# Modulation half vectors on TensorE, four weight chunks at a time in column groups of the array

## The chip, the cores and the metric

One core of a Trainium2 chip runs the whole program. The metric is the device time of one execution in microseconds (us), as the median of several runs. TensorE appears in the profile as PE (matmuls) and PEld (weight loads), VectorE as DVE, ScalarE as ACT, GpSimd as POOL, and SyncE, which issues most transfers, as SP.

## The reference

Two layers over 512 latent tokens and 256 context tokens of width 1024. Every sub-layer norms its input, multiplies by one plus a scale vector and adds a shift vector; those vectors ("modulation") come from a conditioning vector c through one large matrix, once for the latents and once for the context.

```python
silu_c = jax.nn.silu(c)
silu_cc = jax.nn.silu(c_ctx)
for i in range(DEPTH):
    m_lat = (silu_c @ ada_w[i] + ada_b[i]).reshape(b, N_SUBLAYERS, N_MOD, 1, d)
    m_ctx = (silu_cc @ ada_w[i] + ada_b[i]).reshape(N_SUBLAYERS, N_MOD, 1, d)
    h = norm_modulate(x_lat, norm_g[i, 0], m_lat[:, 0, 0], m_lat[:, 0, 1])
    x_lat = x_lat + MACARON_WEIGHT * m_lat[:, 0, 2] * swiglu(h, ffn_w_in[i, 0], ffn_w_out[i, 0])
```

After the first feed-forward come a token mixer (a short convolution in layer 0, attention in layer 1) and a second feed-forward. The output is a final norm of the latent tokens. All data are float32.

## The kernel before

Tokens lie along the free dimension and the 1024 features along the partitions, in 8 chunks of 128 (`KC`). Each weight and each normed activation is split into a high and a low float32r part (`split`, L178 on ACT and L179 on DVE), and a product is three matmuls (`mm3`, L388 to L390): high by high, high by low, low by high. Normed activations are the tiles `h` (high) and `hl` (low), weights `wh` and `wl`, cut from a landed block `raw`.

A modulation vector has 1024 entries and is made as two halves of 512, numbered `hm`; (0,2) and (0,3) are the two halves of layer 0's first scale vector, (0,0) and (0,1) those of its first shift vector. These four are needed before the first norm can end, and are made first:

- `ada_load` (L197 on) issues eight transfers on SP, one weight piece `adw` [128, 512] for each chunk k of c. The pieces share ten buffers in turn, so a later transfer waits until the matmul on the buffer's previous piece is done.
- `ada_direct` (L207 to L218) makes a half on TensorE, for (0,2), (0,0) and (0,3). Eight float32 matmuls (L211) with the activated conditioning vector `silu_c[:, k, :]`, two columns (latents, context), as the stationary operand sum into two rows of one PSUM bank. ACT copies the two rows out (`adr`, L214), four transposes turn them to 128 partitions (L217, PSUM tile `ps_S`, of which there is one buffer), and `ada_put` adds the bias (L193) into `mods`. It is a generator: it yields behind each matmul, and the caller places the steps between other work of TensorE.
- `ada_split` (L226 on) makes (0,1) with its sum over k on DVE (`acc`, L222 and L224), for the latents and then for the context, and sums over partitions with four matmuls against ones (L235).

The order of work in this stretch is written by hand: TensorE's and SP's order is the program order throughout, and DVE's and ACT's too until `boot_order.close()`. The top level runs (0,2) on TensorE, loads x, then the squares of x (L306 to L310), their sum over partitions (L335, L336), the root (`rsqrt`, L318 to L322), with the steps of (0,0) between. Then scale (L341), t = x * scale * r (L361), h (L381, on ACT) and hl (L368) for the first four chunks. The first feed-forward's `first` (its three first chunks of hidden columns) calls `boot` ahead of each of its first eleven steps of three matmuls, which places one matmul of (0,3) before each of the first eight; later calls place the rest of (0,3), the column sums of (0,1), and the whole norm of the context tokens (x of the context is `xc`).

Of the kernel before, what the change touches and what calls it, by code (L numbers as in the profile page):

```python
# [9 lines left out]
F32 = mybir.dt.float32  # L10
F32R = mybir.dt.float32r
BF16 = mybir.dt.bfloat16
AF = mybir.ActivationFunctionType
ALU = mybir.AluOpType
# [3 lines left out]
P = 128  # L18
# [29 lines left out]
def backbone(ctx: ExitStack, tc: tile.TileContext, a: dict, out: bass.AP):  # L48
# [10 lines left out]

    # ---------------------------------------------------------- PSUM  # L60
    bank = {}
# [13 lines left out]

    # ---------------------------------------------------------- constants
    packed = ctile("packed", [P, sum(n for _, n in VECTORS)])
# [29 lines left out]

    # ---------------------------------------------------------- weights
    # Each entry of the stream is one transfer of `units` stationary blocks [P, k chunks, P].
    stream = []  # L110
# [69 lines left out]

    # ---------------------------------------------------------- adaLN vectors
    silu_c = ctile("silu_c", [P, KC, 2])
    ada_tasks = []
    ada_done = set()

    def ada_setup():
        act.activation(silu_c, cvec, AF.Sigmoid)
        dve.tensor_mul(silu_c, silu_c, cvec)

    def ada_put(i, hm, src_ps, vs):  # L190
# [16 lines left out]
    def ada_direct(i, hm, loaded):  # L207
        """Steps of one half vector on TensorE, for the ones that the first norm waits for."""
        ps = ptile("B")
        for k, w in enumerate(loaded):  # L210
            pe.matmul(ps[:2, :], silu_c[:, k, :], w, start=(k == 0), stop=(k == KC - 1))  # L211
            yield
        row = tmp.tile([P, NL], F32, name=f"adr{hm}", tag="t")
        act.activation(row[:2, :512], ps[:2, :], AF.Copy)  # L214
        pt = ptile("S", (P, 4, 2))
        for j in range(4):
            pe.transpose(pt[:, j, :], row[:2, j * P : (j + 1) * P], ident[:2, :2])  # L217
        ada_put(i, hm, pt, range(2))  # L218

# [6 lines left out]
    def ada_split(i, hm, loaded):  # L226
        """A half vector with its sum over k on VectorE, for one token group after the other."""
        acc = apool.tile([P, 2, 512], F32, name=f"acc{i}_{hm}", tag="acc")
        for v in range(2):
            for k, w in enumerate(loaded):  # L230
                ada_add(acc[:, v, :], w, k, v, k == 0)
                yield
            pt = ptile("S", (P, 4, 2))
            for j in range(4):
                pe.matmul(pt[:, j, v : v + 1], acc[:, v, j * P : (j + 1) * P], ones_f, start=True, stop=True)  # L235
            ada_put(i, hm, pt, [v])
            yield
# [47 lines left out]
    def mod_groups(i, m):  # L285
        """Token groups that use modulation vector m of layer i: past the last keys and values, only the latents."""
        return 1 if (i == 1 and m >= 5) else 2
# [4 lines left out]

    # ---------------------------------------------------------- activations
    x_lat = xp.tile([P, KC, NL], F32, name="xl", tag="xl")
# [20 lines left out]
    def rsqrt(r, ps, rows, n, dim):  # L315
        """r = 1/sqrt(ps / dim): the tables' value and one Newton step."""
        y = tmp.tile([P, NL], F32, name="y", tag="t")[:rows, :n]
        act.activation(y, ps, AF.Ln, scale=1.0 / dim)  # L318
        act.activation(y, y, AF.Exp, scale=-0.5)
        dve.tensor_mul(r, y, y)  # L320
        dve.scalar_tensor_tensor(out=r, in0=ps, scalar=-0.5 / dim, in1=r, op0=ALU.mult, op1=ALU.mult)
        dve.scalar_tensor_tensor(out=r, in0=r, scalar=1.5, in1=y, op0=ALU.add, op1=ALU.mult)  # L322

    def parts_of(src, n, dim):
        """src + eps * dim / P, whose sum over the partitions is dim times the mean square plus eps."""
        th = tmp.tile([P, NL], F32R, name="th", tag="th", bufs=1)[:, :n]
# [5 lines left out]
    def rstd_of(th, tl, n, dim, r):  # L332
        """r = 1/sqrt(sum over partitions of th + tl / dim + eps), on every partition."""
        ps = ptile("S")[:, :n]
# [57 lines left out]
    def banks(grp, count, own=False):  # L392
        """PSUM for `count` outputs of one token group."""
        v, off, n = grp
# [9 lines left out]
    def project(grp, units, ps, interleave=False, mid=None, hooks={}):  # L404
        """ps[u] = unit u's columns applied to the normed tokens of one group."""
        v, off, n = grp
# [16 lines left out]
    def out_steps(groups, gh, gl, npart, after):  # L423
        """Steps of x += gate * (w_out applied to the npart chunks in gh/gl).

        `after` is the norm that follows the last part: it starts on the first group while the
        second is still being summed; the second group's norm is left in `pending`."""

# [54 lines left out]

    # ---------------------------------------------------------- sub-layers
    def gated(gp, count, name):
        return ([gp.tile([P, NT], F32R, name=f"{name}{z}{f}", tag=f"g{z}{f}") for f in range(count)] for z in "hl")

    def ffn(gp, i, s, groups, after, boot=None):
# [12 lines left out]
        def first(lat, cxt):  # L501
            """The first three chunks: the latents' part begins with half of the k chunks."""
            units = [w_get(1), w_get(1)]
# [16 lines left out]
        def opening(main, other):  # L520
            """The first three chunks: the main group's part covers the norm of the other group."""
            units = [w_get(), w_get(), w_get()]
# [87 lines left out]
    def attention(gp, i, s, after):  # L610
# [7 lines left out]
        with tc.tile_pool(name="rope", bufs=1) as rp, psum(A=4, B=2, S=1, Q=1):  # L618
# [4 lines left out]
            def turned(dst, p, g, n):  # L623
                """dst = the rotation of p * g; g[:, 1] is g with its halves swapped."""
                w = tmp.tile([P, NL], F32, name="hw", tag="t")[:, :n]
# [36 lines left out]

            # Heads are normed behind their projections, `n` of them in the course of one.
            lat, cxt = BOTH
# [174 lines left out]

    # ---------------------------------------------------------- program  # L840
    for i in range(2):
# [13 lines left out]
    with tc.tile_pool(name="apool", bufs=1) as apool, tc.tile_pool(name="g0", bufs=1) as gp, psum(A=4, B=3, S=1):  # L855
# [4 lines left out]
        scale = ada_direct(0, 2, ada_load(gp, 0, 2))  # L860
        for _ in range(KC):
            next(scale)
# [3 lines left out]
        shift = ada_direct(0, 0, ada_load(gp, 0, 0))  # L866
        for _ in range(3):
            next(shift)
        for m in range(KC):
            sq_add(m, 0, NL)  # L870
        parts = norm_parts(lat)
        r = norm_rstd(lat, *parts)
        for _ in range(3):
            next(shift)
        next(scale, None)
        for _ in range(2):
            next(shift)
        scale_vec(0, 0, slice(0, 4))
# [8 lines left out]
        def boot_steps():  # L887
            scale = ada_direct(0, 3, ada_load(gp, 0, 3))
            shift = ada_load(gp, 0, 1)
            for m in range(KC):  # L890
                nc.sync.dma_start(xc[m], a["x"][m, :, NL:])
            for _ in range(KC):
                next(scale)
                yield
# [55 lines left out]
def _layout(i):  # L950
# [20 lines left out]
    w = arr("attn_w_qkv")[0].reshape(KC, P, 6, 2, P)  # L971
    # The halves that rotate into each other lie 64 partitions apart, both axes in each.
    qk = w.reshape(KC, P, 6, 2, 2, 2, NF).swapaxes(4, 5).reshape(w.shape).transpose(2, 1, 3, 0, 4)
# [27 lines left out]
```

## Time and profile before

| | us |
|---|---|
| median of 3 runs | 2629.04 |
| lowest and highest run | 2628.71, 2629.2 |
| profiled execution, first to last instruction (span) | 2627.3 |
| TensorE busy in it | 2595.5 |
| half vectors made by L211, first to last matmul start | 4.6 to 44.7 |

The profile shows one execution. Its span is 1.7 us under the median of the runs, which holds what lies around the first and last instruction as well. Busy time of TensorE says that it had a matmul in flight, not that the array was full. A float32 matmul appears as two instructions, a float32r matmul as one.

### The profile page before, as it was taken

How to read it: one execution, taken by the hardware profiler on the slowest of the kernel's cores; microseconds unless marked ns; L12 is line 12 of the kernel's file. 1: busy time of each engine (PE TensorE's matmuls, PEld its weight loads, DVE VectorE, ACT ScalarE, POOL GpSimd, SP SyncE). 2: the span in 40 equal slices, each digit the busy share in tenths (PEclk: the TensorE clock that was granted, in tenths of full speed). 3: DMA queues.
4: the chain of work that ended last, by engine and by line, in shares of the span. 5: the costliest groups of instructions: out<-in, count | busy, mean ns of one | idle time of the engine just before them, and what ended most of it. 6: DMA issues, size and time to landing. Idle time of an engine off the chain costs nothing.

```text
span 2627.3 us, 38843 instructions
## 1 busy us (share of the span) xinstructions
PE 2595.5 (99%) x16500; PEld 2302.0 (88%) x16500; DVE 1579.6 (60%) x2692; ACT 870.5 (33%) x1398; POOL 0.7 (0%) x6
## 2 busy tenths in 40 slices
PE   8999999999999999999999999999999999999998
PEld 3888888888888888888888888888888799999998
DVE  6856566569656674555756745443337887644445
ACT  3423222234213432222323422221125785422222
POOL 0000000000000000000000000000000000000000
PEclk9999999999999999999999999999999999999999
DMA  6333232232323032332323233321112201223221
GB/s 242 137 122 106 93 121 97 89 113 74 120 81 121 33 126 86 110 113 97 121 89 125 82 110 108 122 77 53 64 65 73 81 1 34 86 97 107 97 87 43
DMA packets 69566, 249.57 MB, mean 95 GB/s; under 512 B 5776, under 2 KB 8976, under 8 KB 56336
## 3 DMA queue, kind: packets, MB, share of 16 engines
q1 hardware_dynamic: 52112, 184.17, 20.0%
q10 hardware_dynamic: 17280, 62.92, 6.8%
q8 instruction: 129, 2.11, 0.3%
q14 instruction: 45, 0.37, 0.0%
HBM read 244.97 MB, written 2.10 MB: 94 GB/s over the span
## 4 chain that ended last, share of the span: by engine, by line
PE 93%; DVE 4%; ACT 2%; DMA 0%; issue 0%; SPq 0%; DVEq 0%; ACTq 0%
PE ps_A L388 19%; PE ps_A L389 18%; PE ps_A L390 18%; PE ps_B L388 11%; PE ps_B L389 11%; PE ps_B L390 11%; PE ps_S L268 1%; DVE wl L179 1%; DVE hl L368 1%; DVE t L361 1%; PE ps_B L211 1%; ACT pr L764 1%; PE ps_T L780 0%; DVE ssq L310 0%; PE ps_O L390 0%
## 5 line engine op out<-in xcount | busy, mean ns | idle before, releaser
L388 PE MATMUL ps_A<-h,wh 128*128 128x512 f32 (+1 forms) x1624 | 604.5, 372 | 0.3 <-ACT h L381 0.3
L389 PE MATMUL ps_A<-hl,wh 128*128 128x512 f32 (+1 forms) x1624 | 601.7, 370 | 0.4 <-DVE hl L368 0.4
L390 PE MATMUL ps_A<-h,wl 128*128 128x512 f32 (+1 forms) x1624 | 601.7, 370 | 0.1
L178 ACT ACTIVATE wh<-raw 128x1024 fp32r<-128x1024 f32 (+2 forms) x342 | 339.0, 993 | 642.9 <-PE ps_B L389 626.0
L179 DVE TENSOR_TENSOR wl<-raw,wh 128x1024 fp32r<-128x1024 f32 (+2 forms) x342 | 389.5, 1141 | 234.6 <-ACT wh L178 230.7
L388 PE MATMUL ps_B<-h,wh 128*128 128x256 f32 (+1 forms) x1672 | 479.7, 287 | 0.0
L389 PE MATMUL ps_B<-hl,wh 128*128 128x256 f32 (+1 forms) x1672 | 478.4, 286 | 0.4 <-DVE hl L368 0.2
L390 PE MATMUL ps_B<-h,wl 128*128 128x256 f32 (+1 forms) x1672 | 477.6, 286 | 0.0
L388 PEld LDWEIGHTS ps_A<-h,wh 128*128 128x128 f32 x1624 | 305.9, 188 | 60.3 <-issue 6.0
L390 PEld LDWEIGHTS ps_A<-h,wl 128*128 128x128 f32 x1624 | 305.8, 188 | 56.5 <-DVE wl L179 0.6
L389 PEld LDWEIGHTS ps_A<-hl,wh 128*128 128x128 f32 x1624 | 306.0, 188 | 54.5 <-DVE hl L368 1.8
L389 PEld LDWEIGHTS ps_B<-hl,wh 128*128 128x128 f32 x1672 | 314.9, 188 | 5.8 <-DVE hl L368 1.2
L388 PEld LDWEIGHTS ps_B<-h,wh 128*128 128x128 f32 x1672 | 315.1, 188 | 4.6
L390 PEld LDWEIGHTS ps_B<-h,wl 128*128 128x128 f32 x1672 | 315.1, 188 | 2.5
L224 DVE SCALAR_TENSOR_TENSOR acc<-aw,silu_c,acc 128x512 f32<-128x512 f32 x392 | 278.0, 746 | 16.0 <-DMA aw<-in_ada_w 14.6
L388 PE MATMUL ps_A<-gh,wh 128*128 128x512 f32 (+1 forms) x704 | 255.8, 363 | 0.0
L389 PE MATMUL ps_A<-gl,wh 128*128 128x512 f32 (+1 forms) x704 | 255.7, 363 | 0.0
L390 PE MATMUL ps_A<-gh,wl 128*128 128x512 f32 (+1 forms) x704 | 255.3, 363 | 0.0
L441 DVE SCALAR_TENSOR_TENSOR xl<-ps_A,gat,xl 128x512 f32<-128x512 f32 (+1 forms) x192 | 126.5, 671 | 203.2 <-PE ps_A L390 203.1
L390 PE MATMUL ps_B<-gh,wl 128*128 128x256 f32 x704 | 199.2, 283 | 0.0
L389 PE MATMUL ps_B<-gl,wh 128*128 128x256 f32 x704 | 199.2, 283 | 0.0
L388 PE MATMUL ps_B<-gh,wh 128*128 128x256 f32 x704 | 199.1, 283 | 0.0
(203 smaller groups left out, 3103.2 us busy)
## 6 DMA issues: line engine op xcount, KB each, us to landing
raw<-in_ffn_w_in SPq DMA_DIRECT2D x88, 1024.0 KB, 4.8
aw<-in_ada_w ACTq DMA_DIRECT2D x120, 512.0 KB, 3.2
raw<-in_ffn_w_out SPq DMA_DIRECT2D x24, 1024.0 KB, 4.9
raw<-in_ffn_w_out SPq DMA_DIRECT2D x32, 640.0 KB, 3.9
adw<-in_ada_w SPq DMA_DIRECT2D x32, 256.0 KB, 5.4
raw<-in_conv_w_in SPq DMA_DIRECT2D x8, 1024.0 KB, 4.9
raw<-in_attn_w_qkv SPq DMA_DIRECT2D x6, 1024.0 KB, 4.8
aw<-in_ada_w SPq DMA_DIRECT2D x8, 512.0 KB, 3.4
```

Of the source, the lines that this page charges most:

```text
L178: act.activation(dsth, src, AF.Copy)
L179: dve.tensor_tensor(out=dstl, in0=src, in1=dsth.bitcast(F32), op=ALU.subtract)
L211: pe.matmul(ps[:2, :], silu_c[:, k, :], w, start=(k == 0), stop=(k == KC - 1))
L224: dve.scalar_tensor_tensor(out=acc, in0=w, scalar=silu_c[:, k, v : v + 1], in1=acc, op0=ALU.mult, op1=ALU.add)
L268: pe.matmul(pt[:, j, v : v + 1], pc[:, j * P : (j + 1) * P], ones_b, start=(n == 0), stop=(n == 2))
L361: dve.scalar_tensor_tensor(out=t, in0=xs(m, off, n), scalar=scl[:, m, v : v + 1], in1=r, op0=ALU.mult, op1=ALU.mult)
L368: dve.scalar_tensor_tensor(out=hl[m][:, off : off + n], in0=t, scalar=mods[i][:, 3 * s, m, v : v + 1], in1=hs.bitcast(F32), op0=ALU.add, o ...
L388: pe.matmul(ps, wh, xh, start=first, stop=False)
L389: pe.matmul(ps, wh, xl, start=False, stop=False)
L390: pe.matmul(ps, wl, xh, start=False, stop=last)
L441: dve.scalar_tensor_tensor(out=x, in0=p[:, :n], scalar=gat[:, m0 + u, v : v + 1], in1=x, op0=ALU.mult, op1=ALU.add)
L764: act.activation(pr, sc, AF.Exp, bias=sm[:, 1:2], scale=rq[:, blk, h : h + 1], accum_out=sm[:, 2:3])
```

## The change

`silu_c` is copied into a zeroed tile `silu_p` [128, 8, 32], which borrows the buffer of the last low part `hl7`. `ada_direct` gives the matmul of chunk k the 32 array columns from 32 * (k % 4) on, so that it writes the 32 rows of the same number in PSUM; chunks k and k + 4 sum into the same rows. It yields after four matmuls instead of one. ACT copies all 128 rows, four full 128x128 transposes turn them, a reduce on DVE adds the four partial sums (columns 32 g + c for the two c), and `ada_put` adds the bias from that sum. The callers take a step where they took four.

```diff
     def ada_setup():
         act.activation(silu_c, cvec, AF.Sigmoid)
         dve.tensor_mul(silu_c, silu_c, cvec)
+        silu_p.append(xp.tile([P, KC, 32], F32, name="silu_p", tag="hl7"))
+        dve.memset(silu_p[0], 0.0)
+        dve.tensor_copy(silu_p[0][:, :, :2], silu_c)
...
         ps = ptile("B")
         for k, w in enumerate(loaded):
-            pe.matmul(ps[:2, :], silu_c[:, k, :], w, start=(k == 0), stop=(k == KC - 1))
-            yield
+            g = 32 * (k % 4)
+            pe.matmul(ps[g : g + 32, :], silu_p[0][:, k, :], w, start=(k < 4), stop=(k >= 4), tile_position=(0, g), skip_group_check=True)
+            if k % 4 == 3:
+                yield
         row = tmp.tile([P, NL], F32, name=f"adr{hm}", tag="t")
-        act.activation(row[:2, :512], ps[:2, :], AF.Copy)
-        pt = ptile("S", (P, 4, 2))
+        act.activation(row, ps, AF.Copy)
+        pt = ptile("S", (P, 4, P))
         for j in range(4):
-            pe.transpose(pt[:, j, :], row[:2, j * P : (j + 1) * P], ident[:2, :2])
-        ada_put(i, hm, pt, range(2))
+            pe.transpose(pt[:, j, :], row[:, j * P : (j + 1) * P], ident)
+        sums = tmp.tile([P, 4, 2], F32, name=f"ads{hm}", tag="ads", bufs=1)
+        dve.tensor_reduce(out=sums, in_=pt.rearrange("p j (g c) -> p j c g", g=4)[:, :, :2, :], axis=AX.X, op=ALU.add)
+        ada_put(i, hm, sums, range(2))
...
-        for _ in range(KC):
+        for _ in range(2):
             next(scale)
...
-        for _ in range(3):
-            next(shift)
+        next(shift)
         for m in range(KC):
             sq_add(m, 0, NL)
         parts = norm_parts(lat)
         r = norm_rstd(lat, *parts)
-        for _ in range(3):
-            next(shift)
         next(scale, None)
-        for _ in range(2):
-            next(shift)
+        next(shift)
...
-            for _ in range(KC):
-                next(scale)
+            for k in range(KC):
+                if k % 4 == 3:
+                    next(scale)
                 yield
```

Line numbers move by 4 from `ada_load` on and by 8 behind `ada_direct`: L211 becomes L216, the transposes L217 become L223, the reduce is L225, L335 is L343, and L388 to L390 are L396 to L398.

The first place is TensorE's queue around the sum of squares (L335, L336), where the names are those of the sections above. Before:

```order
L211 MATMUL ps_B<-adw_2_161,silu_c 2x512
L335 MATMUL ps_S<-th,ones_r 128x512
L336 MATMUL ps_S<-tl,ones_r 128x512
L211 MATMUL ps_B<-adw_3_163,silu_c 2x512
L211 MATMUL ps_B<-adw_4_165,silu_c 2x512
L211 MATMUL ps_B<-adw_5_167,silu_c 2x512
L217 MATMUL ps_S<-ident,adr_216 128x2 x4
L211 MATMUL ps_B<-adw_6_169,silu_c 2x512
L211 MATMUL ps_B<-adw_7_171,silu_c 2x512
L217 MATMUL ps_S<-ident,adr_233 128x2 x4
```

The same place now:

```order
L216 MATMUL ps_B<-adw_2_164,silu_p 32x512
L216 MATMUL ps_B<-adw_3_166,silu_p 32x512
L343 MATMUL ps_S<-th,ones_r 128x512
L344 MATMUL ps_S<-tl,ones_r 128x512
L223 MATMUL ps_S<-ident,adr_217 128x128 x4
L216 MATMUL ps_B<-adw_4_168,silu_p 32x512
L216 MATMUL ps_B<-adw_5_170,silu_p 32x512
L216 MATMUL ps_B<-adw_6_172,silu_p 32x512
L216 MATMUL ps_B<-adw_7_174,silu_p 32x512
L223 MATMUL ps_S<-ident,adr_238 128x128 x4
```

The matmul of k=3 has moved ahead of the sum of squares, and those of k=4 and k=5 behind the transposes of (0,2).

The second place is TensorE's queue in the first chunk of the feed-forward, where (0,3) is worked in. Before, from the first matmul of (0,3):

```order
L211 MATMUL ps_B<-adw_0_298,silu_c 2x512
L388 MATMUL ps_A<-h_252,wh_0_244 128x512
L389 MATMUL ps_A<-hl_253,wh_0_244 128x512
L390 MATMUL ps_A<-h_252,wl_0_245 128x512
L211 MATMUL ps_B<-adw_1_300,silu_c 2x512
L388 MATMUL ps_A<-h_252,wh_1_246 128x512
L389 MATMUL ps_A<-hl_253,wh_1_246 128x512
L390 MATMUL ps_A<-h_252,wl_1_247 128x512
L211 MATMUL ps_B<-adw_2_302,silu_c 2x512
```

Now, from the end of the third step of three:

```order
L396 MATMUL ps_A<-h_259,wh_0_251 128x512
L397 MATMUL ps_A<-hl_262,wh_0_251 128x512
L398 MATMUL ps_A<-h_259,wl_0_252 128x512
L216 MATMUL ps_B<-adw_0_305,silu_p 32x512
L216 MATMUL ps_B<-adw_1_307,silu_p 32x512
L216 MATMUL ps_B<-adw_2_309,silu_p 32x512
L216 MATMUL ps_B<-adw_3_311,silu_p 32x512
L396 MATMUL ps_A<-h_259,wh_1_253 128x512
L397 MATMUL ps_A<-hl_262,wh_1_253 128x512
L398 MATMUL ps_A<-h_259,wl_1_254 128x512
```

Before, one matmul of (0,3) stood ahead of each of the first eight steps; now four stand behind the third step and four behind the seventh. SP's and ACT's queues keep their order, and DVE's gains the memset, the copy and three reduces, each directly ahead of the adds that it feeds.

More of the change, by code (lines that the diff above doesn't have):

```diff
@@ L182, in backbone @@
     silu_c = ctile("silu_c", [P, KC, 2])
+    silu_p = []
     ada_tasks = []
```

## The prediction

> **What bounds the kernel now.** I read the page first, for the engine that sets the end.
>
> ```profile
> span 2627.3 us, 38843 instructions
> PE 2595.5 (99%) x16500; PEld 2302.0 (88%) x16500; DVE 1579.6 (60%) x2692; ACT 870.5 (33%) x1398; POOL 0.7 (0%) x6
> PE 93%; DVE 4%; ACT 2%; DMA 0%; issue 0%; SPq 0%; DVEq 0%; ACTq 0%
> ```
>
> The third line is the chain of work that ended last: TensorE nearly throughout. A microsecond taken from TensorE's queue therefore comes off the end, unless another chain is then late at a later join. The change touches only the first 50 us, so next I read the timeline of that stretch (start, length, engine, line, operation; in brackets the idle time before it and what ended it).
>
> ```profile
> 12.01 5.12 SPq L203 DMA_DIRECT2D adw<-in_ada_w  x8
> 17.46 4.42 PE L211 MATMUL ps_B<-adw,silu_c 128*2 128x512 f32 x6 [4.36 <-DMA adw<-in_ada_w]
> 21.81 0.50 PE L335 MATMUL ps_S<-th,ones_r 128*128 128x512 f32 x1
> 22.47 2.74 PE L211 MATMUL ps_B<-adw,silu_c 128*2 128x512 f32 x6
> 25.50 0.38 PE L217 MATMUL ps_S<-ident,adr 2*128 2x2 f32 x4 [0.29 <-DVE r L321]
> 25.80 1.88 PE L211 MATMUL ps_B<-adw,silu_c 128*2 128x512 f32 x4
> 27.78 0.59 ACT L214 ACTIVATE adr<-ps_B 2x512 f32<-2x512 f32 x1 [3.40 <-PE ps_B L211]
> 28.42 0.40 PE L217 MATMUL ps_S<-ident,adr 2*128 2x2 f32 x4 [0.74 <-ACT adr L214]
> 28.86 0.23 DVE L193 TENSOR_TENSOR mods<-ps_S,packed 128x4 f32<-128x4 f32 x2 [1.06 <-PE ps_S L217]
> 31.01 0.73 PE L389 MATMUL ps_A<-hl,wh 128*128 128x512 f32 x1 [0.44 <-DVE hl L368]
> ```
>
> Seen here: the shift vector (0,0) is the long chain. Its sums (L211) end at 27.68, then come ACT's copy, the transposes and the add at 28.86; h and hl start from it, and TensorE's steady work from hl at 31.01. Each float32 matmul is two instructions (x6 is three matmuls). Warm, six take 2.74, so their starts lie (2.74-0.59)/5 = 0.43 us apart.
>
> Behind that, the other two vectors share the queue with the first feed-forward chunks.
>
> ```profile
> 35.07 1.02 PE L211 MATMUL ps_B<-adw,silu_c 128*2 128x512 f32 x2
> 36.02 0.50 PE L388 MATMUL ps_A<-h,wh 128*128 128x512 f32 x1
> 36.90 1.02 PE L211 MATMUL ps_B<-adw,silu_c 128*2 128x512 f32 x2
> 38.68 3.90 DVE L224 SCALAR_TENSOR_TENSOR acc<-adw,silu_c,acc 128x512 f32<-128x512 f32 x5
> 39.80 2.17 SPq L203 DMA_DIRECT2D adw<-in_ada_w  x2
> 44.72 0.75 DVE L224 SCALAR_TENSOR_TENSOR acc<-adw,silu_c,acc 128x512 f32<-128x512 f32 x1 [1.05 <-DMA adw<-in_ada_w]
> 47.50 0.40 PE L389 MATMUL ps_A<-hl,wh 128*128 128x512 f32 x1
> 47.73 0.39 PE L390 MATMUL ps_A<-h,wl 128*128 128x512 f32 x1
> 47.96 0.95 PE L235 MATMUL ps_S<-ones_f,acc 128*128 128x1 f32 x8
> 48.77 0.48 PE L388 MATMUL ps_A<-h,wh 128*128 128x512 f32 x1
> ```
>
> An f32r matmul costs TensorE 47.73-47.50 = 0.23. One step with a modulation matmul takes 36.90-35.07 = 1.83, so that matmul costs 1.83-3x0.23 = 1.14, of which 0.86 is its own two instructions and the rest the turn to and from it. Between 31 and 46 us TensorE carries seven of them. At 47.96 it reaches the column sums of vector (0,1) (L235), whose sum DVE finished at 44.72+0.75 = 45.47: there is 2.4 us of room for TensorE to come earlier before it must wait for DVE. DVE in turn waited for the last weight piece, which SP issues at 39.80+2.17-0.33 = 41.64, when the k=5 matmul of (0,3) frees its buffer.
>
> The granted clock is the third thing that carries the sum.
>
> ```profile
> 17.46:20.87 3.41, 3.41 (x5) 0.50 (x6) 2.01 (x3) 0.72 (x1) 0.00 (x0) 0.50 1.06 398
> 20.87:31.11 10.24, 8.47 (x27) 2.07 (x25) 6.05 (x15) 5.04 (x10) 0.00 (x0) 1.00 1.02 399
> 31.11:34.53 3.42, 3.42 (x6) 0.96 (x7) 3.29 (x6) 1.57 (x4) 0.00 (x0) 0.50 0.54 198
> 34.53:44.77 10.24, 10.24 (x30) 3.11 (x28) 8.48 (x12) 2.27 (x3) 0.00 (x0) 1.00 0.47 160
> ```
>
> The number before the last two is the clock: half in 17.46 to 20.87 and again in 31.11 to 34.53, full otherwise. It changes on a grid of 3.41 us, so every cold matmul here costs twice the warm one, and how busy TensorE is in one such stretch settles the next.
>
> **The change, part by part.** *Setup.* A memset of 128x256 and a small copy on DVE, between the silu product and the first matmul.
>
> ```profile
> 0.83 0.17 DVE L90 MEMSET ones_r<- 128x128 f32 x1 [0.83 <-PEq L990]
> 3.00 0.18 DVE L188 TENSOR_TENSOR silu_c<-silu_c,packed 128x16 f32<-128x16 f32 x1 [1.80 <-ACT silu_c L187]
> 4.55 8.54 PE L211 MATMUL ps_B<-adw,silu_c 128*2 128x512 f32 x16 [4.55 <-DMA adw<-in_ada_w]
> ```
>
> Twice the memset plus a copy like L188 is 0.34+0.18 = 0.52, from 3.18 to 3.7; the first matmul waits for its weights until 4.55. Cost 0; it would show only from 0.85 us more.
>
> *A group of four matmuls.* No row of before has column groups, so I bound it. Above: nothing overlaps, eight starts, 8x0.43 = 3.44 warm. Below: the four run side by side, 2x0.43 = 0.86. I take the middle case: TensorE starts its instructions in program order in all these rows, and a matmul's second instruction starts 0.43 after its first into the same rows of PSUM; the next matmul's first can therefore run beside the previous one's second, not earlier. That makes five steps, 5x0.43 = 2.15 warm, plus 0.10 at each turn (36.02-35.07-2x0.43 = 0.09 today). [...]
>
> *Row, transposes, reduce.* ACT copies 128 rows rather than 2, the transposes are 128x128, and a reduce stands ahead of the adds.
>
> ```profile
> 83.49 0.58 ACT L494 ACTIVATE sg<-ps_A 128x512 f32<-128x512 f32 x1
> 2100.45 0.88 PE L780 MATMUL ps_T<-ident,pr 128*128 128x128 f32 x6 [0.47 <-ACT pr L767]
> L780 PE MATMUL ps_T<-ident,pr 128*128 128x128 f32 x192 | 27.8, 275 | 1.8 <-DVE p L179 1.1 <-ACT pr L767 0.5
> L729 DVE TENSOR_SCALAR rq<-ps_S 128x32 f32<-128x32 f32 x1 | 0.2, 184 | 0.0
> ```
>
> The copy costs the same (0.58 against 0.59). Six transposes take 0.88, so four take 0.275+3x0.12 = 0.64 against 0.40: +0.24. The reduce reads the 32 columns that L729 reads: 0.18, with the step to the next dependent instruction 0.22; its bounds are 0.16 (the small adds) and 0.4. So a vector's end lies 0.46 us further behind its last matmul.
>
> *Up to hl.* L335 now stands behind four matmuls of (0,0), not three. The k=3 weights are there at about 17.46+3x0.68 = 19.5 (eight issues in 5.12, 0.68 apart, the first in at 17.46). At the cold clock the starts in five steps are 17.46, 18.3, 19.1, 20.0, 20.83, and L335 follows at 21.4, 0.4 before today. The transposes of (0,2) wait for r as today, 25.1. Then k=4..7 of (0,0) all stand behind them: from 25.7, last start 27.4, end 28.0 (27.68 today). Copy, transposes, reduce: the adds begin at 28.0+0.10+0.59+0.05+0.64+0.04+0.22 = 29.6, **0.75 late**. DVE's work from there to the sum of (0,1) is one row of instructions, and slips with it; TensorE's hl starts at 31.76.
>
> *Up to the column sums.* Eight f32r matmuls, cold until 34.53 (0.43 each, 6.5 of them), then warm: 34.9. First group of (0,3): 0.1+4x0.43+0.53 = 2.35, to 37.2; twelve f32r matmuls, 2.8, to 40.0; second group, to 42.4; three more, then the transposes behind ACT's copy at 43.15, to 43.7; six more, 45.1. The k=5 matmul ends at 40.1+0.86+0.59 = 41.55, so the last piece of (0,1) is issued when it is today (41.64) and DVE's sum ends at 45.4. L235 starts at 45.45 rather than 47.96: **2.5 us early**, with DVE and TensorE now meeting there.
>
> *What is late next.* Two things could eat this.
>
> ```profile
> 45.88 0.36 SPq L149 DMA_DIRECT2D raw<-in_ffn_w_in  x1
> DMA to landing us min/median/max: 7.2/7.5/9.0
> 53.96 1.99 ACT L178 ACTIVATE wh<-raw 128x1024 fp32r<-128x1024 f32 x2
> 64.72 0.48 DVE L329 SCALAR_TENSOR_TENSOR tl<-ssq,eps,th 128x256 fp32r<-128x256 f32 x1
> 67.10 0.28 PE L336 MATMUL ps_S<-tl,ones_r 128*128 128x256 f32 x1
> 79.72 0.39 PE L389 MATMUL ps_B<-hl,wh 128*128 128x256 f32 x1 [0.17 <-DVE hl L368]
> ```
>
> The third weight block stands behind the (0,1) pieces and x of the context on SP, all issued as today, and lands at 45.88+7.5 = 53.4. ACT's split of it at 53.96 can move up 0.6 only, and with it DVE's second sum and tl, which ends at 65.20. L336 needs tl and stands at 67.10: 1.9 of room and 0.6 moved. So 2.5 passes, with nothing to spare; I take **2.4**. The context's norm (to 79.72) hangs on TensorE's second column sums and on itself and moves whole, and so does all behind it.
>
> **Sum.** 2627.3 - 2.4 = 2624.9 us of span. The median of the runs is 1.7 above this execution's span, so 2629.04 - 2.4 = 2626.6.
>
> **Rivals.** *No overlap in the array: slower.* Place: the second half of (0,0). With eight starts a group, L335 is 0.86 late (two more instructions, warm by then), the transposes start at 26.3, the second group at 26.95 and its end is 30.55 against 27.68; the adds begin at 32.2, hl at 34.3. TensorE is then mostly idle in 31.11 to 34.53 and stays cold one more stretch, to 37.94: eight f32r to 37.75, group 3.6 to 41.4, twelve to 44.2, group to 47.8, transposes behind the copy 49.2, six to 50.6, sums done at 51.4 against 48.77: +2.6, **2631.6**. It decides from a group cost of about 2.8 us on. For it: every L211 row today keeps 0.43 between starts; against it: the groups write different rows of PSUM. A dearer turn than the 0.10 of today adds to this case: an L211 ends 0.59-0.43 = 0.16 after the next one's start, and if each turn waits for that end, the six turns into and out of the last three groups add about 6x0.16 = 0.9, to 2632.5. [...]
>
> *Side by side, 0.86 a group.* L335 at 21.1, second group of (0,0) ends at 26.5, the adds come 0.7 early; the groups of (0,3) end by 38.5 and DVE's row alone sets L235: the sum of (0,1) can start at 37.5, eight dependent steps of (3.90-0.75)/4 = 0.79 end it at 43.6. Resumed at 44.5: -4.2; the third block is issued 3.5 early and no longer clips it. **2624.8.** [...]
>
> **How the numbers follow.** Five steps 0.50 (2626.6); no overlap, with or without drains, 0.28 (2631.6 to 2632.5); side by side 0.15 (2624.8); anything else, a stretch of clock lost or a wait I don't see, 0.07. All three named cases are to be held: the range is 2624.4 to 2632.5, the ends being the third case with 0.4 for the reduce and the clock's grid, and the drains. The likeliest case's own range is 2625.5 to 2628 (one more stretch of 3.41 us at half clock costs TensorE 1.7, less the 0.35 that it waits at L235: 1.4). A measurement of this kernel tells 0.2%, 5.3 us, from no change; 2623.8 and 2634.3 are those bounds, and no case reaches them: faster 0.03, same 0.92, slower 0.05.
>
> **What would show it.** In the profile after: the starts inside a group of eight L216 instructions (about 0.43 apart in pairs for five steps, singly for none, bunched for side by side); the adds of the shift vector at 29.6; hl at 31.8; no idle of more than 0.5 before the column sums, which start at 45.5; a clock of 0.50 for one stretch after 31.1. I am wrong if the groups keep eight even starts, if the clock stays at 0.50 past 34.6, or if TensorE waits for tl at L344.

## The result, and the profile after

The changed kernel takes 2639.40 us (median of 5 runs, 2638.27 to 2640.0), the kernel before 2628.71 in 5 runs beside it: 10.7 us slower, a ratio of 1.0039 with a 95% interval of 1.0027 to 1.0051. The forecast was 2626.6, and 2639.4 lies above the range of 2624.4 to 2632.5. The page of the profile after, by the lines that were shown of before:

```profile
span 2638.0 us, 38847 instructions
PE 2600.7 (99%) x16500; PEld 2311.0 (88%) x16500; DVE 1581.5 (60%) x2697; ACT 871.8 (33%) x1398; POOL 0.7 (0%) x6
PE 93%; DVE 4%; ACT 2%; DMA 1%; issue 0%; SPq 0%; DVEq 0%; ACTq 0%
```

TensorE still sets the end, with the same 16,500 instructions, and it is busy 5.2 us longer although the change took work off it. By the difference of span and busy time it also waits 5.5 us longer (37.3 against 31.8). So the loss is not one late chain. The timeline of the first 50 us shows what the change did where it was made:

```profile
20.68 0.79 PE L343 MATMUL ps_S<-th,ones_r 128*128 128x512 f32 x1
24.85 0.80 PE L223 MATMUL ps_S<-ident,adr 128*128 128x128 f32 x4 [2.95 <-DVE r L329]
25.58 1.93 PE L216 MATMUL ps_B<-adw,silu_p 128*32 128x512 f32 x8
28.37 1.12 PE L223 MATMUL ps_S<-ident,adr 128*128 128x128 f32 x4 [0.86 <-ACT adr L220]
29.75 0.24 DVE L197 TENSOR_TENSOR mods<-ads,packed 128x4 f32<-128x4 f32 x2
31.90 0.79 PE L397 MATMUL ps_A<-hl,wh 128*128 128x512 f32 x1 [0.39 <-DVE hl L376]
39.22 0.40 PE L398 MATMUL ps_A<-h,wl 128*128 128x512 f32 x1
39.55 1.06 PE L216 MATMUL ps_B<-adw,silu_p 128*32 128x512 f32 x8
40.54 0.50 PE L396 MATMUL ps_A<-h,wh 128*128 128x512 f32 x1
43.15 0.40 PE L398 MATMUL ps_A<-h,wl 128*128 128x512 f32 x1
44.05 1.54 DVE L232 SCALAR_TENSOR_TENSOR acc<-adw,silu_c,acc 128x512 f32<-128x512 f32 x2 [0.58 <-DMA adw<-in_ada_w]
45.74 1.87 PE L243 MATMUL ps_S<-ones_f,acc 128*128 128x1 f32 x8 [2.20 <-DVE ads L225]
```

Eight instructions, a group of four float32 matmuls, take 1.06 us from the first start to the last end (39.55). With one instruction lasting 0.59 that leaves 0.47 between the first and the last start: the four run side by side. In the trace their first instructions start at 39.55 to 39.57, 0.007 apart, and their second ones at 40.00 to 40.02: no second instruction holds back the first of the next matmul. From L398 at 39.22 to L396 at 40.54 a visit costs 1.32-0.23 = 1.09, of which 0.86 is the group. The column sums start at 45.74, against 47.96 before: 2.2 us early. But TensorE had waited 2.20 for them: DVE's sum ends at 44.05+1.54 = 45.59, and the reduce of (0,3) behind it, which frees the one `ps_S` buffer, 0.1 later. And they take 1.87 instead of 0.95. The reason for that is in the stretches of the clock (the number before the last two):

```profile
14.95:21.77 6.82, 4.82 (x10) 1.23 (x10) 3.82 (x6) 2.63 (x5) 0.00 (x0) 0.50 1.06 414
21.77:25.19 3.42, 0.47 (x4) 0.37 (x4) 1.83 (x3) 1.71 (x3) 0.00 (x0) 1.00 1.00 420
25.19:35.43 10.24, 7.76 (x24) 3.75 (x22) 7.99 (x20) 5.03 (x9) 0.00 (x0) 0.50 0.69 254
35.43:45.67 10.24, 8.12 (x42) 4.42 (x41) 9.26 (x13) 2.87 (x4) 0.00 (x0) 1.00 0.70 208
45.67:52.50 6.83, 6.75 (x20) 5.69 (x21) 5.17 (x13) 2.58 (x4) 0.00 (x0) 0.50 0.86 277
```

Behind the stretch in which TensorE is busy 0.47 of 3.42 us the clock is at 0.50 for three stretches of 3.41 us, where before it was so for one; and behind the wait for the column sums it is at 0.50 for two more, 45.67 to 52.50, which did not exist before. Laying the TensorE instructions of the two traces beside each other in order, the same instruction stands 2.2 us early at the column sums and 1.0 late at 52.3. The gain of the boot (the work up to here, ahead of the steady matmuls) is gone there.

From 52 us on it is 1.0 us late, then evenly later up to the attention: 1.3 at 186 us, 2.9 at 799, 5.0 at 1498 and 6.5 at 2021; at 2580 it is 10.6. Nothing in the diff runs there, and between 60 and 2000 us TensorE waits 0.2 us in all, before 0.35. The groups of matmuls by shape show it. Before (the last number ahead of the second bar is the mean length in ns):

```profile
L388 PE MATMUL ps_A<-h,wh 128*128 128x512 f32 x1272 | 505.5, 397 | 0.3 <-ACT h L381 0.3
L390 PE MATMUL ps_A<-h,wl 128*128 128x512 f32 x1272 | 502.6, 395 | 0.1
L388 PE MATMUL ps_A<-gh,wh 128*128 128x512 f32 x528 | 206.0, 390 | 0.0
L388 PE MATMUL ps_B<-h,wh 128*128 128x256 f32 x1616 | 457.5, 283 | 0.0
```

And after:

```profile
L396 PE MATMUL ps_A<-h,wh 128*128 128x512 f32 x1272 | 507.9, 399 | 1.2 <-ACT h L389 1.2
L398 PE MATMUL ps_A<-h,wl 128*128 128x512 f32 x1272 | 505.3, 397 | 0.0
L396 PE MATMUL ps_A<-gh,wh 128*128 128x512 f32 x528 | 205.9, 390 | 0.0
```

The 512-wide matmuls on h are 2 ns longer, those on g (the gated hidden columns, the operand of the second product) are not. And one thing stood in the profile of before already: the same shape, with weights from the same buffers, takes 390 ns on g and 395 to 397 on h.

One difference between the programs is not in any line that runs there. The new tile `ads` (8 floats, 32 bytes in each partition) lies in the pool ahead of the weight buffers, so that, by the order and the sizes of the tiles in the program, `raw`, `wh`, `wl`, the attention's tiles and g lie 32 bytes higher in SBUF. And `silu_p` takes the buffer of `hl7` before any part of h is allocated, so that the eight h and seven other hl lie 3072 bytes higher.

### The profile page after: what moved, and what is told of

The parts are those of the page before. It is cut to its first block, busy times and chain, and to the rows that moved or that the text cites. A ratio compares the mean times of both kernels' runs of the same rounds, so it can differ in the third digit from the quotient of the medians.

```text
span 2638.0 us, 38847 instructions
## 1 busy us (share of the span) xinstructions
PE 2600.7 (99%) x16500; PEld 2311.0 (88%) x16500; DVE 1581.5 (60%) x2697; ACT 871.8 (33%) x1398; POOL 0.7 (0%) x6
## 3 DMA queue, kind: packets, MB, share of 16 engines
q1 hardware_dynamic: 52112, 184.17, 20.4%
## 4 chain that ended last, share of the span: by engine, by line
PE 93%; DVE 4%; ACT 2%; DMA 1%; issue 0%; SPq 0%; DVEq 0%; ACTq 0%
PE ps_A L396 19%; PE ps_A L398 18%; PE ps_A L397 18%; PE ps_B L396 11%; PE ps_B L397 11%; PE ps_B L398 11%; PE ps_S L276 1%; DVE wl L179 1%; DVE hl L376 1%; DVE t L369 1%; PE ps_T L788 1%; ACT pr L772 1%; DMA adw<-in_ada_w 0%; DVE ssq L318 0%; PE ps_B L216 0%
## 5 line engine op out<-in xcount | busy, mean ns | idle before, releaser
L396 PE MATMUL ps_A<-h,wh 128*128 128x512 f32 (+1 forms) x1624 | 606.7, 374 | 1.2 <-ACT h L389 1.2
L398 PE MATMUL ps_A<-h,wl 128*128 128x512 f32 (+1 forms) x1624 | 604.6, 372 | 0.0
L179 DVE TENSOR_TENSOR wl<-raw,wh 128x1024 fp32r<-128x1024 f32 (+2 forms) x342 | 389.9, 1142 | 237.9 <-ACT wh L178 234.3
L396 PE MATMUL ps_B<-h,wh 128*128 128x256 f32 (+1 forms) x1672 | 479.9, 287 | 0.0
L398 PE MATMUL ps_B<-h,wl 128*128 128x256 f32 (+1 forms) x1672 | 476.5, 285 | 0.0
L398 PEld LDWEIGHTS ps_A<-h,wl 128*128 128x128 f32 x1624 | 305.9, 188 | 59.0 <-DVE wl L179 0.4
L396 PEld LDWEIGHTS ps_A<-h,wh 128*128 128x128 f32 x1624 | 306.7, 189 | 56.2 <-issue 1.7
L396 PEld LDWEIGHTS ps_B<-h,wh 128*128 128x128 f32 x1672 | 314.5, 188 | 4.7
L398 PEld LDWEIGHTS ps_B<-h,wl 128*128 128x128 f32 x1672 | 315.9, 189 | 2.5
L396 PE MATMUL ps_A<-gh,wh 128*128 128x512 f32 (+1 forms) x704 | 255.7, 363 | 0.0
L398 PE MATMUL ps_A<-gh,wl 128*128 128x512 f32 (+1 forms) x704 | 255.4, 363 | 0.0
L398 PE MATMUL ps_B<-gh,wl 128*128 128x256 f32 x704 | 199.2, 283 | 0.0
L396 PE MATMUL ps_B<-gh,wh 128*128 128x256 f32 x704 | 199.1, 283 | 0.0
```

The lines of the kernel that those rows point to most:

```text
L179: dve.tensor_tensor(out=dstl, in0=src, in1=dsth.bitcast(F32), op=ALU.subtract)
L396: pe.matmul(ps, wh, xh, start=first, stop=False)
L398: pe.matmul(ps, wl, xh, start=False, stop=last)
```

## The experiments

Times are medians, and each difference is against the kernel before run on the same chip beside it (2628.35 us in the first set, 2628.68, 2627.18 and 2628.66 in the others). The ratios compare means, so they can differ a little from the medians.

### First set: is it the place in SBUF?

**Theory A** was that the even loss comes from where the tiles lie; **rival B** that it comes from the column groups or the clock. `e1_place_back` is the changed kernel with all tiles of h, hl and weights at the addresses of before:

```diff
+        for m in range(KC):
+            if m % 2 == 0:
+                xp.tile([P, 2, NT], F32R, name=f"h{m // 2}", tag=f"h{m // 2}")
+            if m < KC - 1:
+                xp.tile([P, NT], F32R, name=f"hl{m}", tag=f"hl{m}")
         silu_p.append(xp.tile([P, KC, 32], F32, name="silu_p", tag="hl7"))
...
-        sums = tmp.tile([P, 4, 2], F32, name=f"ads{hm}", tag="ads", bufs=1)
+        sums = tmp.tile([P, 4, 2], F32, name=f"ads{hm}", tag="st", bufs=4)
```

> The change as it is, except that every tile of h, hl and of the weights lies at the SBUF address that it has in the kernel before (buffers are only taken in another order; no instruction differs). Theory A (the loss behind 53 us, about 8 us, comes from where the tiles lie, and the boot comes out at about +0.9 us because the clock falls to 0.50 in the new idle gaps): the even drift between 53 and 2014 us is gone, the time is 2628 to 2632 us, and the boot still ends about 0.9 us late at 52.3. Rival B (the loss comes from the column groups or the clock, and placement is without weight): 2637 to 2641 us, and the even drift stays.

Measured: 2629.63 us, ratio 1.0006 (0.9997 to 1.0015). In its profile, which is of the longest of the eleven executions, the same instruction is 2.8 us late at 54.2 us, where 0.9 was expected, and still 2.7 at 912: the even loss is gone, and what is left is the boot.

`e2_h_moved`, `e3_w_moved` and `e4_both_moved` are the kernel before with one line, or both; no instruction differs:

```diff
+        xp.tile([P, NT], F32R, name="pad_h", tag="hl7")
...
+        tmp.tile([P, 4, 2], F32, name=f"ads{hm}", tag="ads", bufs=1)
```

The first line stands in `ada_setup` (e2), the second in `ada_direct` (e3).

> The kernel before, with the tiles of h and hl at the addresses that they have in the changed kernel (3072 bytes higher; hl7 first); no instruction differs. Theory A with the h tiles as the cause: 2634 to 2637 us, with the mean of the 128x512 matmuls on h by 0.5 ns or more longer. Theory A with the weights as the cause, or rival B: 2628 to 2630 us.

Measured: 2628.48 us, ratio 1.0001 (0.9992 to 1.0009). The 3072 bytes cost nothing.

> The kernel before, with the weight buffers (raw, wh, wl), sm, the attention's tiles and g at the addresses that they have in the changed kernel (32 bytes higher); no instruction differs. Theory A with the weights as the cause: 2634 to 2637 us. Theory A with the h tiles as the cause, or rival B: 2628 to 2630 us.

Measured: 2635.98 us, ratio 1.0034 (1.0021 to 1.0046): 7.6 us from 32 unused bytes.

> The kernel before, with both moves of addresses at once; no instruction differs. Theory A: 2635 to 2638 us, the even drift of the changed kernel in it without any change of the boot. Rival B: 2628 to 2630 us.

Measured: 2636.03 us, ratio 1.0033 (1.002 to 1.0045). Rival B has fallen: the even loss stands in kernels that have no column groups, and its size is that of e3. With 7.6 from the place of the weights and 1.3 from e1, 8.9 of the 10.7 us are accounted for; each of the three numbers is uncertain by 2 to 3 us, so the rest is within that. (By the means it is 8.8 and 1.7 of 10.5.)

### Second set: what about the place, and what of the boot?

`e5_w_by_64` has the pad of e3 at 64 bytes (`[P, 4, 4]`). `e7_all_by_32` has a pad of 32 bytes ahead of h, which moves h, the temporaries and the weights alike; `e6_h_by_32` has that and e3's, so that h moves by 32 and the weights by 64:

```diff
+    xp.tile([P, 8], F32, name="pad_x", tag="pad_x")
```

> The kernel before with the same buffers moved as in the run with +32 bytes, but by 64 bytes, so that they lie at an odd multiple of 32 bytes again as in the kernel before (in that run they lay at a multiple of 64). Theory A64 (what counts is the address modulo 64 bytes): 2628 to 2630 us. Rival (any other place of the buffers costs): 2633 us or more.

Measured: **2607.76 us**, ratio 0.9929 (0.9911 to 0.9947). Both theories fell: not the address modulo 64, and another place need not cost. It gains 20.9 us. (One of its four executions took 2617.01, which pulls the ratio up.)

> The kernel before with h, hl and the temporary tiles moved by 32 bytes (to multiples of 64), the weight buffers by 64 (still at odd multiples of 32). If the weights' address modulo 64 alone counts: 2628 to 2630 us. If it counts that h and the weights differ modulo 64: 2635 to 2638 us. If h at a multiple of 64 costs or gains by itself, it shows here: any other time.

Measured: 2637.42 us, ratio 1.0034 (1.0021 to 1.0048).

> The kernel before with everything from h on moved by 32 bytes: h, hl, the temporaries and the weight buffers all lie at multiples of 64. If the weights' address modulo 64 alone counts: 2635 to 2638 us. If it counts that h and the weights differ modulo 64: 2628 to 2630 us.

Measured: 2627.46 us, ratio 0.9996 (0.9987 to 1.0006). The three together point to one reading: it is the **distance** between h and the weights that counts. Moved together, nothing clear of the noise (e7); apart by 32 bytes, 8 to 9 us slower, whether reached by e3 or by e6; apart by 64, 21 us faster.

`e8_place_back_fill` is e1 with TensorE kept busy in its five longest gaps of the start by transposes whose results nobody reads:

```diff
+        spare = ptile("A")
+
+        def fill(n, ps=spare):
+            for q in range(n):
+                pe.transpose(ps[:, q % 4 * P : (q % 4 + 1) * P], ident, ident)
+
+        fill(36)
...
+        fill(22)
...
+        fill(5)
...
+        fill(8)
...
+            fill(26, ptile("B"))
```

> The change with the addresses of before (as in the first run), and with 97 transposes of the identity into a spare bank put on TensorE in its five longest gaps of the start: 36 before the first group of (0,0), 22 before the transposes of (0,2), 5 before those of (0,0), 8 before the first matmul on h, 26 before the column sums of (0,1). Theory C (the boot's gain is given back because the clock falls to 0.50 after the gaps): the clock keeps 1.0 through 30 to 52 us, the boot ends 2 to 4 us earlier than before at 52 us, and the time is 2624.5 to 2627.5 us. Rival (the boot is held by the transfers and VectorE, whatever the clock): 2628.5 to 2631 us, with the clock at 1.0 and the same waits.

Measured: 2625.16 us, ratio 0.9986 (0.9976 to 0.9995); 4.8 us under e1 by the differences. Its stretches and the steps of the boot:

```profile
8.25:25.19 16.94, 14.98 (x87) 8.48 (x90) 7.74 (x12) 7.48 (x12) 0.00 (x0) 1.00 1.04 382
25.19:35.43 10.24, 9.03 (x52) 5.39 (x45) 9.39 (x21) 6.92 (x11) 0.00 (x0) 1.00 0.88 320
45.67:52.50 6.83, 6.83 (x31) 5.52 (x31) 6.38 (x9) 5.41 (x10) 0.00 (x0) 1.00 0.60 233
```

```profile
26.94 0.66 PE L228 MATMUL ps_S<-ident,adr 128*128 128x128 f32 x4 [0.16 <-ACT adr L225]
30.01 0.50 PE L402 MATMUL ps_A<-hl,wh 128*128 128x512 f32 x1 [0.69 <-DVE hl L381]
39.97 3.00 PE L884 MATMUL ps_B<-ident 128*128 128x128 f32 x26
43.32 1.05 PE L248 MATMUL ps_S<-ones_f,acc 128*128 128x1 f32 x8 [0.34 <-DVE ads L230]
```

The clock stays at 1.00; the transposes of (0,0) take 0.66 instead of 1.12, hl comes at 30.01 instead of 31.90, the column sums start at 43.32 instead of 45.74 and take 1.05 instead of 1.87. Behind the column sums the same instruction stands 4.5 us early against the profile of before, a little over the 2 to 4 expected, where by 52 it stood 1.0 late in the changed kernel. The timed executions agree: the mean granted clock is 0.993 to 0.994 in all five of the changed kernel and 0.994 to 0.996 in those of e1, against 0.997 to 0.998 in those of e8. Theory C holds in that the clock took what the boot had gained. How much of the 4.5 us is the groups' and how much the fillers' is the question of the fourth set.

### Third set: which buffers, which distance?

h and hl tiles begin at multiples of 512 bytes from the first h, the 128-column blocks of `wh` and `wl` at multiples of 512 from the first `wh`. So the distance between a block and a row of h, modulo 512, is one number for the whole kernel: 128 before, 160 in e3, 192 in e5. For g it is 0 in all of them, since g lies behind the weights in the same order. (These places are worked out from the order and the sizes in which the pools hand out their tiles; no profile shows an address.) `e10_w_by_128` pads by 128 (distance 256). `e11_tmp_ahead` exchanges two pools, which gives 0. `e12_raw_stays` moves all but `raw` by 64:

```diff
-    xp = ctx.enter_context(tc.tile_pool(name="xp", bufs=1))
     tmp = ctx.enter_context(tc.tile_pool(name="tmp", bufs=4))
+    xp = ctx.enter_context(tc.tile_pool(name="xp", bufs=1))
...
         units, todo = [], []
+        if n == 0:
+            wp.tile([P, 16], F32, name="pad_w", tag="pad_w", bufs=1)
```

(The first two edits are e11, the last is e12.)

> The kernel before with the weight buffers, the attention's tiles and g moved by 128 bytes. The distance of the weights from h modulo 512 bytes (all blocks of both begin at multiples of 512 bytes from their first) is then 256, where it was 128 before, 160 in the slow runs and 192 at 2607.76; for g, whose matmuls take 227 to 228 ns, it is 0 in every run. No theory gives the size; theory D (this distance alone sets the pitch of the matmuls on h) says that the time differs from 2628.7 by a change of the pitch on h, with that on g unchanged: 2595 to 2640 us.

Measured: 2614.49 us, ratio 0.995 (0.9935 to 0.9965).

> The kernel before with the pool of the temporary tiles laid ahead of the pool of h, x and the sums (one line moved up; weights, g and the attention's tiles stay): h then lies at a distance of 0 modulo 512 bytes from the weights, as g does. Theory D: the 128x512 matmuls on h come down to the 227 to 228 ns of those on g, from 232.8 to 234.7: 2606 to 2612 us by these alone. Rival (it is the place of the weights against the temporary tiles, or of the weights by itself): 2628 us, or the slow 2636.

Measured: 2614.37 us, ratio 0.9948 (0.9931 to 0.9964). The time missed the 2606 to 2612 that was expected. The groups show why: the 512-wide matmuls did come down nearly to those on g (393 against 397, then 390), the 256-wide ones did not come down (284, before 283).

```profile
L388 PE MATMUL ps_A<-h,wh 128*128 128x512 f32 x1272 | 499.9, 393 | 0.3 <-ACT h L381 0.3
L390 PE MATMUL ps_A<-h,wl 128*128 128x512 f32 x1272 | 495.9, 390 | 0.0
L388 PE MATMUL ps_B<-h,wh 128*128 128x256 f32 x1616 | 459.6, 284 | 0.0
```

In e5 it is the other way: the 256-wide ones gain most.

```profile
L389 PE MATMUL ps_A<-h,wh 128*128 128x512 f32 x1272 | 503.1, 395 | 0.3 <-ACT h L382 0.3
L391 PE MATMUL ps_A<-h,wl 128*128 128x512 f32 x1272 | 501.1, 394 | 0.2 <-DVE wl L179 0.2
L389 PE MATMUL ps_B<-h,wh 128*128 128x256 f32 x1616 | 453.7, 281 | 0.0
```

> The kernel before with 64 bytes put between the raw weights and wh: wh, wl, g and the attention's tiles move by 64, the raw buffers, into which the transfers write, stay. Theory D (TensorE's reads of wh and wl against those of h): 2606 to 2610 us as in the run that moved all by 64. Rival (the writes of the transfers or the reads of raw by ScalarE and VectorE): 2627 to 2630 us.

Measured: 2606.8 us, ratio 0.9922 (0.9907 to 0.9937), as e5. So `raw` and the transfers into it have no part in it; the place of `wh` and `wl` against h has.

`e9_fill_64` joins the two findings: e8 with a 64-byte pad.

> The run with the fillers (2625.16 us) with the weight buffers, the attention's tiles and g moved by a further 64 bytes, as in the run that moved them so in the kernel before (2607.76). Theory D (the two causes are independent: what matters is the distance between h and the weights in SBUF, and the clock in the boot): 2602.5 to 2606.5 us, -3.5 against 2607.76. Rival (the gain of the 64 bytes hung on the boot's phase): over 2608 us.

Measured: **2603.04 us**, ratio 0.9908 (0.9893 to 0.9923): 24 us faster than before, the fastest version of all, and as theory D has it.

```profile
L402 PE MATMUL ps_A<-h,wh 128*128 128x512 f32 x1272 | 501.9, 395 | 0.4 <-ACT h L395 0.4
L402 PE MATMUL ps_B<-h,wh 128*128 128x256 f32 x1616 | 453.2, 280 | 0.0
```

### Fourth set: whose gain is the boot's, and is the distance smooth?

`e13_before_fill` is the kernel before with `fill(36)` ahead of the first matmuls of (0,0) and `fill(5)` ahead of its transposes; `e14_fill_96` is e9 with 96 bytes for 64.

> The kernel before, at its own addresses and with its own modulation matmuls, with fillers in its own long gaps: 36 transposes of the identity before the first matmuls of (0,0), 5 before the transposes of (0,0). It tells what the fillers alone bring. Theory C (the column groups shorten the boot by some 4 us once the clock is held; the fillers alone save no more than the two stretches at 0.50 cost before): 2626 to 2628 us. Rival (all of the 3.5 us comes from the fillers): 2624 to 2625.5 us.

Measured: 2627.02 us, ratio 0.9994 (0.9986 to 1.0003), as theory C has it. Its clock, too, is held (the stretch that was at 0.50 before), and its column sums start at 45.53 where those of e8 start at 43.32:

```profile
31.11:34.53 3.42, 3.42 (x11) 1.12 (x10) 3.29 (x6) 1.90 (x3) 0.00 (x0) 1.00 0.80 280
```

```profile
45.53 0.95 PE L235 MATMUL ps_S<-ones_f,acc 128*128 128x1 f32 x8
```

Against the profile of before, e13 stands 2.4 us early behind the column sums, and e8 2.1 more. By the times it is 1.6 and 1.9, with intervals that overlap (0.9986 to 1.0003 against 0.9976 to 0.9995). Both traces hold the clock there, so the 2.1 are the groups'; that they gain is shown by the traces, how much only roughly.

The fillers' 2.4 is not all theirs, for the profile of before is one draw of several. Of the ten profiles with its modulation matmuls and no fillers, six have a stretch at 0.50 that begins between 29 and 32 us, and four have none, e2 and e7 among them; those two stand 1.9 and 2.3 us early there without a filler. The stretches lie elsewhere against the work in each execution, so the same wait falls into one stretch or is shared by two. Here are the stretches ahead of that place, first of before, then of e2, whose next one stays at 1.00:

```profile
27.70:31.11 3.41, 1.95 (x8) 0.70 (x8) 2.35 (x7) 3.33 (x7) 0.00 (x0) 1.00 1.05 387
27.97:31.38 3.41, 2.58 (x10) 0.96 (x11) 2.88 (x7) 3.35 (x7) 0.00 (x0) 1.00 1.05 387
```

> The run with the fillers and the weights moved by 64 bytes (2603.04 us), with 96 in place of 64: the distance of the weights from h modulo 256 bytes is then 224, between 192 (512-wide matmuls on h 229.8 to 231.8 ns, 256-wide 116.7 to 118.8) and 0 (227.1 to 229.9, 120.1 to 121.3). If the pitch is a smooth function of the distance: 2600 to 2606 us. If it steps with 32 bytes: anything between 2595 and 2635 us.

Measured: 2616.81 us, ratio 0.9958 (0.9944 to 0.9971). Not smooth: 32 bytes more than in e9 cost 12.3 us, by the differences.

The pitch of the matmuls on h (mean ns from one start to the next between 60 and 2000 us, where TensorE does not wait, worked out from the starts in each trace), by the distance modulo 256. The last column but one is what the matmuls on h, all behind 60 us, take more than in the trace of before by their pitch:

| distance | run | 512 wide: h·wh, hl·wh, h·wl | 256 wide: h·wh, hl·wh, h·wl | matmuls on h, us against before | time, us against before |
|---|---|---|---|---|---|
| 0 | e11 | 229.6, 227.8, 227.2 | 121.3, 120.1, 120.0 | -15.3 | -12.8 |
| 0 (256) | e10 | 229.9, 227.6, 227.1 | 121.3, 120.1, 120.0 | -15.3 | -12.7 |
| 128 | before | 234.7, 232.8, 233.0 | 120.6, 119.5, 119.2 | 0 | 0 |
| 128 | e7 | 234.9, 232.9, 233.0 | 120.3, 118.9, 118.8 | -1.6 | -1.2 |
| 160 | changed kernel | 236.6, 231.9, 234.4 | 121.5, 120.9, 119.2 | +8.7 | +10.7 |
| 160 | e3 | 236.4, 232.1, 234.3 | 121.5, 121.0, 119.2 | +8.7 | +7.6 |
| 160 | e6 | 236.8, 234.3, 231.6 | 122.1, 120.2, 119.6 | +8.8 | +8.7 |
| 192 | e5 | 231.8, 229.7, 230.9 | 118.8, 116.8, 116.8 | -21.3 | -20.9 |
| 192 | e12 | 232.0, 229.8, 230.6 | 118.8, 116.9, 116.8 | -21.4 | -20.4 |
| 192 | e9, with fillers | 231.8, 229.8, 230.9 | 118.6, 116.7, 116.7 | -21.7 | -24.1 |
| 224 | e14, with fillers | 235.5, 233.7, 233.4 | 118.3, 117.3, 117.4 | -7.7 | -11.9 |

For the operand g (distance 0) the same means are 228.1, 227.5, 226.7 and 119.7, 119.9, 120.0 before, and within 0.7 ns of that in every run: 0 on h gives what 0 on g gives, but for h·wh at both widths. Equal distances give equal sums, to 1.6 us, by whichever move they were reached, and the sums follow the times to 3 us where there are no fillers. With the distance back at 128, in e1, and unchanged in e2, the sum is within 0.2 us of before. One thing goes against the distance alone: e3 and e6 have the same sum, but share it out differently among the three matmuls (hl·wh 232.1 against 234.3).

## Why the prediction was wrong, point by point

- **Failed: "moves whole, and so does all behind it."** The step took everything behind the first 50 us to be the program of before, shifted. It is the same program with other addresses, and those cost 7.6 us by the times of e3 and 8.7 by the matmuls on h in the changed kernel's own trace: some 70 to 80% of the loss. No term, no rival and no bound spoke of where tiles lie, although the diff showed a new tile and a borrowed buffer. The row that would have warned was in the profile of before: the 128x512 matmul at 390 ns on gh and 397 on h.
- **Failed: one cold stretch, and 2.4 us kept.** The prediction has "a clock of 0.50 for one stretch after 31.1" and names 0.50 past 34.6 as a sign of being wrong. The clock was at 0.50 up to 35.43, and again from 45.67 to 52.50. The column sums did start early, 45.74 against the 45.45 foreseen; from there to 52.3 the low clock took 3.2 us (from 2.2 early to 1.0 late). The prediction counted how busy TensorE would be, but not that a microsecond saved ahead of a wait becomes idle time, and that the clock fell behind stretches with much of it (0.47 us of work in 21.77 to 25.19, with a wait of 2.95; 1.29 in 42.25 to 45.67, with most of the wait of 2.20). It also read the one stretch after 31.1 as a property of the kernel, where other executions of the same instructions (e2, e7) have none. With the gaps filled, e8 kept the gain.
- **Failed: "five steps, 5x0.43 = 2.15 warm."** A group takes 0.86 plus 0.23 for its two turns: the third rival's mechanism, which had a chance of 0.15. The even starts of before, 0.43 apart, were read off matmuls that write the same rows of PSUM; the four of this group, which write different rows, have their first instructions at 39.55 to 39.57 and their second ones at 40.00 to 40.02. The third rival's time was 2624.8; e8, with the addresses of before and the clock held, took 2625.16, with the sum of (0,1) from 37.17 to 43.17 where the rival had 37.5 to 43.6. So its mechanism and its time were right for a boot in which the clock holds; but that took fillers, which the rival did not have.
- **Right by chance: the adds at 29.6 and hl at 31.76.** Measured 29.75 and 31.90. But the group was shorter than foreseen, and the transposes took 1.12 instead of 0.64 at a clock of 0.50 (0.66 in e8 at 1.00).
- **Right:** the setup costs 0 (the memset and the copy end at 3.78, the first matmul starts at 4.36 when its weights land); the 128-row copy 0.58 to 0.60; the reduce 0.18; the turns 0.1 each (39.22 to 39.55 into a group against a pitch of 0.23, 40.02 to 40.54 out of it against 0.43). The drains behind the upper end of the range, 0.16 at each of six turns, are shown by no run. L343 stood at 20.68, 0.7 earlier than foreseen.
- **Wrong way round: "no idle of more than 0.5 before the column sums."** With groups of 1.1 us TensorE is done at 43.55 and waits 2.20 for DVE, whose sum of (0,1) ends at 45.59, near the 45.4 foreseen. The sum itself waits 0.58 for the last weight pieces, and SP issues those at 40.62 and 41.04, when the second group of (0,3) (39.55 to 40.61) frees their buffers. In e8 that group starts at 36.15, and the sum ends at 43.17 without a wait (5.48 for its last seven steps): with TensorE earlier, the pieces were there in time.

## What to carry to other kernels

Before costing a change, list which tiles it adds, borrows or reorders, and hold the addresses of everything else; a new tile of 32 bytes made this kernel 0.3% slower, and one of 64 bytes made it 0.8% faster. Look for one shape that takes two lengths in the profile (here 395 to 397 ns on h, 390 on g): the difference times its count is a first estimate of what a better place may be worth. And where TensorE is made faster ahead of a wait, ask whether the clock survives the longer wait; cheap work in the gap may be needed to keep the gain. Here it fell to 0.50 behind waits of 2.95 and 2.20 us, and stayed at 1.00 in e8 with 97 transposes in the gaps.

## What the runs showed of the hardware that was not expected

- **In these runs the pitch of the matmuls on h went with the distance between h and the weights in SBUF**, the pitch taken from the starts in the traces, the distance worked out from the program. At 512 wide it goes from 227.1 to 236.8 ns, at 256 wide from 116.7 to 122.1, with nothing moved but addresses (and, in e9 and e14, the fillers of the boot); 0 and 256 bytes give the same to 0.3 ns, steps of 32 bytes change it by up to 6 ns and not evenly. Of the five distances tried, the two widths have their best at different ones (512 wide at 0, 256 wide at 192). What makes the difference is not shown: e12 (2606.8 us with `raw` in its place, 2607.76 in e5 with it moved) excludes `raw` and the transfers into it, but the addresses that TensorE's weight loads read and those that the splits write, `wh` and `wl`, moved together in every run. A layout with 0 for the 512-wide and 192 for the 256-wide part of h was not tried.
- **Four float32 matmuls in column groups took the time of one**, 1.06 us against 1.02 for one by itself (36.90 in the timeline of before).
- **The clock fell for less idle time than a whole stretch, and stayed down for three** (25.19 to 35.43, with TensorE busy 7.76 of 10.24 us) **and in e1 for four** (23.65 to 37.30, 10.51 of 13.65). In the trace of before it fell behind stretches at 1.00 with 0.00 and 1.95 us of TensorE work and stayed at 1.00 behind those with 2.46 and more; in that of after it fell behind 0.48, 0.47 and 1.29. In the 16 profiles of this case, from the first recorded stretch of the clock (7 to 10 us) to 60 us and cut at the clock's own grid of 3.41 us, a stretch at 1.00 with 1.38 us or less of TensorE work is followed by one at 0.50 in 15 cases of 15, one with 2.29 us or more never; in between, 1.55 to 2.17, it fell in 6 cases of 11, and what decides there is open. The prediction has how busy TensorE is in a stretch settle the next; outside 1.55 to 2.17 us these traces bear that out for the stretches at 1.00.
- Eleven of the 16 profiled executions, that of after among them, also show one stretch of 3.41 us at 0.50 in the attention, between 2074 and 2107 us, and five do not, before and e1 among them; e2 and e7, which run the instructions of before in its time, have it. Between 2014 and 2099 us after falls 1.6 us behind before, part of it there. It goes by no edit made here, and what decides it is open.
